# A hybrid decoder step: mixer work with 32-column products held for common slots, a fixed PE order, and two decay levels on all 128 keys

## The chip, the cores and the metric

The kernel runs on one core of a Trainium2 chip. The metric is the device time in microseconds (us), the median of several executions. Views of the profile come from one profiled execution. Engines: PE is TensorE's matmul and PEld its weight load, DVE is VectorE, ACT is ScalarE, POOL is GpSimd, SP is SyncE, which issues most of the DMAs. Matmuls of fp32 data appear in the trace as two instructions each.

## The reference, cut to what matters

A layer of a decoder on 256 prompt tokens and 8 new tokens of 8 samples (264 columns), with a model width of 2048:

```python
mod = jax.nn.silu(c) @ p['w_ada'][l] + p['b_ada'][l]
sh1, sc1, gt1, sh2, sc2, gt2 = jnp.split(mod[:, None, :], 6, axis=-1)
h = rmsnorm(x, p['g_pre_mix'][l]) * (1.0 + sc1) + sh1
z = h @ p['w_in'][l]
...
y_a = spatial_gating(u, v, sgu_w_s, sgu_b_s)                      # A
o_hg, S_hg = gated_linear_recurrence(q_hg, k_hg, hi, log_f, s_hg) # B: 8 heads, dk = dv = 128
o_g, S_g = gated_linear_recurrence(q_g, k_g, gv, log_a, s_gla)    # C: 4 heads, dk = 128, dv = 256
...
merged = gates[:, :, 0] * (branches[0] @ p['w_branch'][l, 0])     # and two more
out = merged @ p['w_out'][l]
x = x + gt1 * rmsnorm(out, p['g_post_mix'][l])
h2 = rmsnorm(x, p['g_pre_mlp'][l]) * (1.0 + sc2) + sh2
y2 = jnp.square(jax.nn.relu(h2 @ p['w_mlp_up'][l])) @ p['w_mlp_down'][l]
x = x + gt2 * rmsnorm(y2, p['g_post_mlp'][l])
```

The recurrence within a chunk is an attention matrix `att[t, s] = sum_d q[t, d] k[s, d] exp(b[t, d] - b[s, d])`, with `b` the running sum of the log decays. The outputs are the two activations, the final states of the prompts and the samples' updated states.

## The kernel before

All weights are fp32 in HBM and are streamed once, in blocks of 512 KB, through a ring of six buffers `raw` (L419 loads, three blocks ahead). A block is split in two parts, `whi` by a cast on ACT (L102) and `wlo` by a subtraction on DVE (L99). Its products with the split activations are three to a tile: L459, L460, L461, 128x128 weights by 264 columns; 24 of them make up one block, called a granule here. There are 13,872 of these main products in the program.

Beside them runs background work, written as Python generators that yield a cost after each step. `linear` calls three queues after each granule: `bg` with the mixers (A, then the two HGRN2 groups of four heads, then GLA), `bs` with the samples' state steps, `ba` with the rounds of the adaLN modulation. Each queue is pumped by a rate, so many steps to a granule:

```python
            bg.pump(rate[0])
            bs.pump(rate[1])
            ba.pump(rate[2])
```

The framework's scheduler then orders the instructions of each engine, PE's too, by its own estimates, within what data and buffers allow.

The pieces that the change touches:

- An adaLN step (`ada_round`, L265) multiplies the condition vectors by two blocks of `w_ada` of 512 KB each, in four products of 512 columns. They use the same `raw` ring. Of the two loads for the next step, one stands ahead of the step's products and one behind them.
- `mixer_r` builds the attention matrix by halving: five small levels within 32 tokens (`small_level`, L852, products of 32 keys by 32 queries), then halves of 32 (L908, 16 products of 32 by 32 a group) and of 64 (L916, 8 products of 64 by 64), then halves of 128 (L935). Behind that stand transposes of the keys (L942), the final states (L950, L951), the outputs (L973, L975, L976), each head's norm (L981, L987) and the transposes back to features (L995).
- `samples_r` advances the samples: it loads a state tile, scales it on ACT (L791), adds the outer product on DVE (L793), stores it from POOL's queue, and multiplies it by the query (L799, four products side by side in PE's column groups for HGRN2, two half sets for GLA).
- `finish(i)` drains what is left of a group and transposes the samples' outputs (L1008). `parts_b` calls it for the two HGRN2 groups, `parts_c` for GLA. `branch` calls these for its first tile, behind the projection of its gates (`zin`).

Of the kernel before, what the change touches and what calls it, by code (L numbers as in the profile page):

```python
# [15 lines left out]
P = 128  # L16
# [20 lines left out]
ST_BUFS = 3  # L37
# [9 lines left out]
FILL = (5.0, 9.0)  # L47


@with_exitstack  # L50
def hybrid_step_kernel(
# [53 lines left out]
    # ---------------------------------------------------------------- constants  # L105
# [7 lines left out]
    # ---------------------------------------------------------------- small vectors  # L113
# [7 lines left out]
    # x: prompt rows as two token tiles, the samples' feature tiles as rows  # L121
# [38 lines left out]
    # ---------------------------------------------------------------- norm helpers  # L160
    def rstd_small(ms, scale, out):
        """out = (ms * scale + EPS) ** -0.5, ms one piece or more of out's columns: a first guess from the exponent's bits, then Newton's steps to float32."""
        n, w = out.shape
        xx, aa = tmp([P, 16], "sx")[0:n, 0:w], tmp([P, 16], "sa")[0:n, 0:w]
        c = 0
        for m in ms if isinstance(ms, list) else [ms]:
            V.tensor_scalar(xx[:, c:c + m.shape[1]], m, scale, EPS, ALU.mult, ALU.add)
            c += m.shape[1]
        V.tensor_scalar(out.bitcast(I32), xx.bitcast(I32), -0.5, 1597463007.0, ALU.mult, ALU.add)
        for _ in range(3):  # L170
            mul(aa, out, out)
            V.scalar_tensor_tensor(aa, aa, -0.5, xx, ALU.mult, ALU.mult)
            V.scalar_tensor_tensor(out, aa, 1.5, out, ALU.add, ALU.mult)

    def sum_features(v, n, w):
        """Sums of v [P, n, w], which it overwrites, over its features (partitions and n tiles), on every partition."""
        while n > 1:
            n //= 2
            add(v[:, 0:n, :], v[:, 0:n, :], v[:, n:2 * n, :])
        ps = sm([P, w])  # L180
# [3 lines left out]
    # ---------------------------------------------------------------- x normed and transposed  # L184
    def norm_rows(x, xs, xsn, r):
        """r [P, 2] = the prompt rows' 1 / rms; xsn = the samples' rows xs [P, KT, NS] over their rms."""
# [7 lines left out]
        ps = sum_features(sq, KT, NS)  # L194
# [5 lines left out]
    def transposed(x, k):  # L200
        """Columns of feature tiles k and k + 1 of the prompt rows, in PSUM [P, 2, NP]."""
# [29 lines left out]
    # ---------------------------------------------------------------- adaLN  # L231
# [6 lines left out]
    def ada_rows(acc, n):  # L238
        """PSUM rows (32 j + c, columns) -> [P, i, j, c] with the columns' features on the partitions."""
        am = tmp([P, 512], "am", 1)  # L240
        S.copy(am[:, 0:n], acc[:, 0:n])
        ps = sm()
# [4 lines left out]
    def ada_round(r, pre=()):  # L247
        """Part r of the modulation; pre are its first blocks of weights."""
# [12 lines left out]
        for k in range(KT):  # L261
            if k + 1 < KT:
                ws.append(load(2 * k + 2))
            for j in range(4):
                T.matmul(acc[32 * j:32 * j + 32, :], cT[:, k, :], ws[j // 2][:, j % 2 * 512:j % 2 * 512 + 512], start=k == 0, stop=k == KT - 1)  # L265
            del ws[0:2]
            if k + 1 < KT:
                ws.append(load(2 * k + 3))
            yield
        rows = ada_rows(acc, 512)  # L270
        yield
        ch = slice(r * KT, (r + 1) * KT)
# [6 lines left out]

    class Queue:  # L280
        """Generators that advance a given number of steps, of any size, at a time."""

        def __init__(self):
            self.g, self.owed = [], 0.0

        def pump(self, n=1.0):
            self.owed += n
            while self.g and self.owed > 0.0:
                try:
                    c = next(self.g[0])  # L290
                    self.owed -= 1.0 if c is None else c
                except StopIteration:
                    self.g.pop(0)
            if not self.g:
                self.owed = 0.0

        def drain(self, gen=None):
            while self.g and (gen is None or gen in self.g):
                try:
                    next(self.g[0])  # L300
                except StopIteration:
                    self.g.pop(0)
# [24 lines left out]
    def ada_first(k0, n):  # L327
        """Shift and scale of the first sub-layer for n feature tiles, and those tiles' activations."""
# [18 lines left out]
        rows = ada_rows(acc, n * 64)  # L347
# [22 lines left out]
    # ---------------------------------------------------------------- streamed product  # L370
# [9 lines left out]
    def plan():  # L380
        """Every block of weights (matrix, row tile, row tiles, column, columns) in the order of use."""
# [28 lines left out]
    class Stream:  # L410
        """The blocks of weights, loaded LOAD_AHEAD and split SPLIT_AHEAD blocks before their products."""
# [36 lines left out]
    def granule(w, k0, n, c0, width, accs, xh, xl, k, first, last):  # L448
        """accs += (rows of w)^T @ x over n feature tiles: w's from k0 + k on, x's from k on, 256 columns to an acc."""
# [13 lines left out]

    def new_acc():
        return pmm.tile([P, 2, 512], F32, tag="mm", name=nm("mm"))

    def linear(w, k0, nk, c0, width, xh, xl):
        """PSUM tile [P, width // P, NT] = (rows k0.. of w, columns c0..c0+width)^T @ x."""
        acc = new_acc()
        kc = min(nk, 1024 // width)  # L470
        for kb in range(0, nk, kc):
            granule(w, k0, kc, c0, width, [acc], xh, xl, kb, kb == 0, kb + kc == nk)
            bg.pump(rate[0])
            bs.pump(rate[1])
            ba.pump(rate[2])
# [19 lines left out]
    # the first columns, by feature tiles as their activations become known  # L495
# [39 lines left out]
    def to_tokens(vt):  # L535
        """[P, 2, >= NP] feature rows of the prompt -> PSUM [P, t, m, P] token rows."""
# [6 lines left out]
    def rows_of(blks, prompt):  # L543
        """Feature rows (pairs of tiles) to the prompt's token rows: prompt(t, g) is the place of pair g."""
# [7 lines left out]
    def sample_rows(blks, eng=None):  # L552
# [7 lines left out]
        return ps  # L560

    # ---------------------------------------------------------------- A: spatial gating
    def mixer_a():
# [9 lines left out]
        for gg in range(2):  # L573
# [4 lines left out]
            mul(wsT[:, 4 * gg:4 * gg + 4, :], ps.rearrange("p (g n) -> p g n", g=4), triu.unsqueeze(1).to_broadcast([P, 4, P]))  # L578
        ps = sm()
# [18 lines left out]
        # the samples' rows, by feature  # L598
# [6 lines left out]
        ps = sum_features(w8, 8, NS)  # L605
# [4 lines left out]
        ps = sum_features(w8, 8, NS)  # L610
        yield 0.4
# [5 lines left out]
        V.tensor_copy(vbk.rearrange("p b k -> p k b"), vs)  # L617
        ps = sm([64, P])
        T.transpose(ps, vbk.rearrange("p b k -> p (b k)"), ident)
        yield 0.9  # L620
        so = tmp([64, P], "vso", 1)
# [9 lines left out]
        for gp in range(4):  # L631
# [14 lines left out]
            yield  # L646
    gen_a = mixer_a()
# [4 lines left out]
    def lower_bounds():  # L652
        """Logs of the lower bounds and of one less them."""
# [16 lines left out]
    def log_sigmoid(out, z, a):  # L670
        """out = log(sigmoid(z)), through a."""
# [9 lines left out]
    # ---------------------------------------------------------------- gated linear recurrences  # L681
# [7 lines left out]
    def hg_group(i):  # L689
        """Four HGRN2 heads."""  # L690
# [37 lines left out]
    def gla_group():  # L728
# [3 lines left out]
        wup = blk([16, 512])  # L732
# [8 lines left out]
        lr = tmp([16, NT], "lr", 1)  # L741
        S.copy(lr, z[0:16, 0, :])
        for m in range(4):
            ps = sm()
            T.matmul(ps[:, 0:NT], wup[:, m * P:(m + 1) * P], lr, start=True, stop=True)
            V.tensor_scalar(G.g[:, m, :], ps[:, 0:NT], bupT[:, m:m + 1], None, ALU.add)
        for s in range(4):
            z = zin(7168 + s * CW)
            S.copy(pair(G.v[s // 2], s % 2), z)
        G.s_in = lambda b, h, n: state_gla[0, b, h:h + n].rearrange("h k v -> k h v")  # L750
# [11 lines left out]
    def samples_r(G):  # L762
        """The samples' one step: S' = f S + k v^T, o = S'^T q."""
# [21 lines left out]
        os_ = tmp([P, dv], f"os{G.i}", 1)  # L785
        for n, (b, h0) in enumerate(steps):
# [7 lines left out]
            nc.gpsimd.dma_start(G.s_out(b, h0, nh), st)  # L794
            yield 0.5
            ps = sm([P, dv])
            for i in range(nh):
                h = h0 + i
                T.matmul(ps[32 * h:32 * h + 32, :], qm[:, h, b, :], st[:, i, :], start=True, stop=True)  # L799
            rs = slice(32 * h0, 32 * (h0 + nh))  # L800
            if b == 0:
                V.tensor_copy(os_[rs], ps[rs])
            else:
                add(os_[rs], os_[rs], ps[rs])
# [8 lines left out]
    def mixer_r(G):  # L813
# [10 lines left out]
        ps = sample_rows(G.v)  # L824
        yield 0.2
        vs = tmp([32 * nj, P], "vso", 1)
        S.copy(vs, ps)
# [10 lines left out]
        # prompts: decays by halving, every exponent at most 0  # L838
# [18 lines left out]

        ps = small_level(k, q)
        yield
        put_level(5, ps)  # L860
        for li, m in enumerate(LEVELS):
# [16 lines left out]
            yield  # L878
            ps = small_level(e, e)
# [7 lines left out]
        # halves of 32 and of 64  # L887
        for m in (32, 64):
# [13 lines left out]
            yield  # L902
            if m == 32:
                ps = sm([P, 8, 32])
                for h in range(4):
                    for b in range(4):
                        r_ = 64 * (b % 2)
                        T.matmul(ps[r_:r_ + 32, 2 * h + b // 2, :], e[:, h, 64 * b:64 * b + 32], e[:, h, 64 * b + 32:64 * b + 64], start=True, stop=True)  # L908
                yield
                S.copy(att[0:32, :, 32:64], ps[0:32])  # L910
                S.copy(att[64:96, :, 96:128], ps[64:96])
# [384 lines left out]
```

## Time and profile before

| | |
|---|---|
| median of 3 runs | 2009.66 us (2008.1 to 2011.21) |
| profiled execution, its span | 2009.9 us |
| PE busy | 1948.6 us (97%) |
| DVE busy, ACT busy | 1191.6 us (59%), 1002.0 us (50%) |
| DMA | 442.05 MB, 220 GB/s |
| main products L459, L460, L461 | 1332.1, 1321.9, 1317.3 us of PE, overlapping |
| adaLN steps L265 | 75.6 us of PE |
| stretch 270 to 980 us (mixers, branches) | PE busy 689.23 us, clock 0.98 |

Matmuls are pipelined, so busy times of groups on PE overlap and add up to more than the span. In a group's row stand the count, the busy time, the mean of one in ns, and the idle time of the engine ahead of it with what ended it. In a row of the timeline, the start and the length come first, and an idle time with its releaser may stand at the end in brackets.

### The profile page before, as it was taken

What the parts mean: (1) busy time and instruction counts of PE and PEld (TensorE: products, weight loads), DVE (VectorE), ACT (ScalarE), POOL (GpSimd) and SP (SyncE); (2) the same over time, 40 slices, a digit from 0 to 9 for tenths busy, and PEclk for the clock granted to TensorE, in tenths of its full rate; (3) what the DMA queues carried; (4) which work ended last, traced back from release to release, by engine and by line L of the source; (5) the groups of instructions that cost most, each with busy time, mean ns of one, the idle gap of its engine ahead of it and who ended that gap; (6) DMA issues with size and microseconds to landing.
All of it is one profiled execution on the core that took longest, in us unless ns stands there. A gap on an engine that the chain in (4) does not pass through costs nothing.

```text
span 2009.9 us, 42161 instructions
## 1 busy us (share of the span) xinstructions
PE 1948.6 (97%) x17020; PEld 1814.9 (90%) x17020; DVE 1191.6 (59%) x2105; ACT 1002.0 (50%) x1773; POOL 40.5 (2%) x66
## 2 busy tenths in 40 slices
PE   5999999999999999899899999999999999999997
PEld 4779898989988987789899995999999999999996
DVE  3456566777475687445555556555555555555656
ACT  4434354576664574454444445555444445454543
POOL 1000000000000000000000000000000000000000
PEclk9999999999999999999999999999999999999998
DMA  9887978787798668887555866655555555555552
GB/s 311 289 300 244 292 229 250 219 276 222 255 286 280 211 207 255 271 273 228 189 179 180 271 200 231 212 185 179 180 183 182 181 179 184 179 183 180 180 179 84
DMA packets 378179, 442.05 MB, mean 220 GB/s; under 512 B 14914, under 2 KB 339136, under 8 KB 377984
## 3 DMA queue, kind: packets, MB, share of 16 engines
q1 hardware_dynamic: 372592, 424.27, 66.7%
q0 software_dynamic: 4496, 13.90, 1.9%
q8 instruction: 133, 2.18, 0.4%
q10 hardware_dynamic: 896, 1.19, 0.2%
q14 instruction: 62, 0.51, 0.1%
HBM read 427.60 MB, written 11.70 MB: 219 GB/s over the span
## 4 chain that ended last, share of the span: by engine, by line
PE 91%; DMA 4%; DVE 2%; ACT 2%; issue 1%; SPq 0%; ACTq 0%; DVEq 0%
PE mm L459 28%; PE mm L460 27%; PE mm L461 27%; PE ada L265 3%; DMA st<-in_state_gla_dram 2%; PE ada L236 2%; DMA raw<-in_w_ada_dram 1%; PE sm L540 1%; PE sm L799 1%; DVE wlo L99 1%; ACT whi L102 1%; DMA raw<-in_w_in_dram 1%; PE sm L852 1%; DMA st<-in_state_hgrn_dram 0%; DMA b<-in_g_post_mix_dram 0%
## 5 line engine op out<-in xcount | busy, mean ns | idle before, releaser
L459 PE MATMUL mm<-b,whi 128*128 128x264 f32 x4624 | 1332.1, 288 | 17.3 <-ACT b L102 8.0
L460 PE MATMUL mm<-b,whi 128*128 128x264 f32 x4624 | 1321.9, 286 | 1.5 <-DVE b L99 1.5
L461 PE MATMUL mm<-b,wlo 128*128 128x264 f32 x4624 | 1317.3, 285 | 3.2 <-DVE wlo L99 3.2
L99 DVE TENSOR_TENSOR wlo<-raw,whi 128x512 fp32r<-128x512 f32 x1156 | 790.6, 690 | 654.1 <-ACT whi L102 616.3
L102 ACT CAST whi<-raw 128x512 fp32r<-128x512 f32 x1156 | 709.1, 619 | 799.5 <-PE mm L460 720.8
L459 PEld LDWEIGHTS mm<-b,whi 128*128 128x128 f32 x4624 | 873.4, 189 | 78.6 <-issue 31.4
L461 PEld LDWEIGHTS mm<-b,wlo 128*128 128x128 f32 x4624 | 872.8, 189 | 13.4 <-issue 7.2
L460 PEld LDWEIGHTS mm<-b,whi 128*128 128x128 f32 x4624 | 873.4, 189 | 11.4 <-issue 8.8
L96 DVE TENSOR_TENSOR b<-b,mm 128x528 f32<-128x528 f32 x136 | 94.9, 698 | 17.8 <-PE mm L461 17.7
L265 PE MATMUL ada<-raw,cT 128*32 128x512 f32 x464 | 75.6, 616 | 3.0 <-DMA raw<-in_w_ada_dram 3.0
L791 ACT ACTIVATE st<-st,fs 128x128 f32<-128x128 f32 (+1 forms) x96 | 37.0, 430 | 69.9 <-DMA st<-in_state_gla_dram 46.3
L793 DVE SCALAR_TENSOR_TENSOR st<-vbc,b,st 128x128 f32<-128x128 f32 (+1 forms) x96 | 33.9, 390 | 62.1 <-ACT st L791 49.0
L236 PE MATMUL ada<-raw,cT 128*32 128x256 f32 (+1 forms) x640 | 43.9, 359 | 3.0 <-DMA raw<-in_w_ada_dram 3.0
L93 DVE TENSOR_TENSOR b<-b,b 128x512 f32<-128x512 f32 (+1 forms) x47 | 33.7, 739 | 2.0 <-ACT b L869 1.6
L794 POOL DMA_DIRECT2D out_dram<-st x32 | 23.5, 736 | 411.0 <-DVE st L793 381.8
L236 PEld LDWEIGHTS ada<-raw,cT 128*32 128x32 f32 x640 | 14.8, 113 | 13.5 <-DMA raw<-in_w_ada_dram 3.7
L265 PEld LDWEIGHTS ada<-raw,cT 128*32 128x32 f32 x464 | 12.2, 110 | 15.7 <-DMA raw<-in_w_ada_dram 6.6
L99 DVE TENSOR_TENSOR b<-gt,b 128x528 fp32r<-128x528 f32 x32 | 22.6, 708 | 3.2
L93 DVE TENSOR_TENSOR gt<-vt 128x528 f32<-128x528 f32 x32 | 22.4, 700 | 0.0
L99 DVE TENSOR_TENSOR b<-b 128x1024 f32<-128x1024 f32 (+1 forms) x21 | 22.3, 1064 | 0.1
L1202 ACT ACTIVATE b<-vt 128x528 fp32r<-128x528 f32 x32 | 20.7, 647 | 1.0
L1196 ACT ACTIVATE vt<-mm 128x528 f32<-128x528 f32 x32 | 19.4, 607 | 0.0
(284 smaller groups left out, 729.5 us busy)
## 6 DMA issues: line engine op xcount, KB each, us to landing
raw<-in_w_in_dram SPq DMA_DIRECT2D x242, 512.0 KB, 5.3
raw<-in_w_ada_dram SPq DMA_DIRECT2D x164, 512.0 KB, 5.2
raw<-in_w_mlp_up_dram SPq DMA_DIRECT2D x128, 512.0 KB, 3.8
raw<-in_w_mlp_down_dram SPq DMA_DIRECT2D x128, 512.0 KB, 3.6
raw<-in_w_branch_dram SPq DMA_DIRECT2D x48, 512.0 KB, 5.1
raw<-in_w_out_dram SPq DMA_DIRECT2D x32, 512.0 KB, 4.3
raw<-in_w_ada_dram SPq DMA_DIRECT2D x32, 256.0 KB, 5.6
vbc<-vs_d SPq DMA_DIRECT2D x32, 256.0 KB, 6.7
```

The costliest lines, as they stand in the source:

```text
L93: V.tensor_tensor(o, a, b, op=ALU.mult)
L96: V.tensor_tensor(o, a, b, op=ALU.add)
L99: V.tensor_tensor(o, a, b, op=ALU.subtract)
L102: S.copy(hi, src)
L236: T.matmul(acc[32 * j:32 * j + 32, 0:n], cT[:, k, :], w[:, n * j:n * j + n], start=k == 0, stop=k == KT - 1)
L265: T.matmul(acc[32 * j:32 * j + 32, :], cT[:, k, :], ws[j // 2][:, j % 2 * 512:j % 2 * 512 + 512], start=k == 0, stop=k == KT - 1)
L459: T.matmul(o, a, xh(k + j), start=first and j == 0, stop=False)
L460: T.matmul(o, a, xl(k + j), start=False, stop=False)
L461: T.matmul(o, b, xh(k + j), start=False, stop=last and j == n - 1)
L791: S.activation(st[:, i, :], st[:, i, :], AF.Copy, scale=fs[:, h0 + i, b:b + 1])
L793: V.scalar_tensor_tensor(st[:, i, :], v[:, i, :], k[:, h0 + i, NP + b:NP + b + 1], st[:, i, :], ALU.mult, ALU.add)
L794: nc.gpsimd.dma_start(G.s_out(b, h0, nh), st)
```

## The change

PE's order is fixed from mixer A to the end of the third branch (`tc.manual_schedule`): PE runs the instructions in the order in which the program is written. The queues get two marks that a generator can yield. At READY it stops until at least one granule has gone by. At NARROW, ahead of products on 32 columns (small levels, sample steps), it stops until a slot comes:

```diff
+NARROW, READY = object(), object()
+SLOT_OWED = 1.0
+SLOT_LATE = 1.9
+SLOT_WAIT = 3
+HELD_OWED = 2.0
...
+    def background():
+
+        now[0] += 1
+        bg.pump(rate[0])
+        bs.pump(rate[1])
+        ba.owed = ba.owed + rate[2] if ba.g else 0.0
+        held = [q for q in (bg, bs) if q.open(NARROW)]
+        if ba.owed >= SLOT_LATE or held and (not ba.g or ba.owed >= SLOT_OWED or now[0] - min(q.at for q in held) >= SLOT_WAIT):
+            bg.slot()
+            bs.slot()
+            ba.pump(0.0)
...
         def pump(self, n=1.0):
             self.owed += n
-            while self.g and self.owed > 0.0:
...
+            while self.g and self.owed > 0.0 and (self.held is None or self.open(READY)):
+                self.step()
             if not self.g:
                 self.owed = 0.0
+            if self.held is not None:
+                self.owed = min(self.owed, HELD_OWED)
...
         for k in range(KT):
-            if k + 1 < KT:
-                ws.append(load(2 * k + 2))
             for j in range(4):
                 T.matmul(acc[32 * j:32 * j + 32, :], cT[:, k, :], ws[j // 2][:, j % 2 * 512:j % 2 * 512 + 512], start=k == 0, stop=k == KT - 1)
-            del ws[0:2]
-            if k + 1 < KT:
-                ws.append(load(2 * k + 3))
-            yield
...
+            ws = [load(2 * k + 2), load(2 * k + 3)] if k + 1 < KT else []
+            yield
...
-ST_BUFS = 3
+ST_BUFS = 4
...
+            sts.append(st)
             yield 0.5
+            if h0 + nh < 4:
+                continue
+            yield NARROW
             ps = sm([P, dv])
-            for i in range(nh):
-                h = h0 + i
-                T.matmul(ps[32 * h:32 * h + 32, :], qm[:, h, b, :], st[:, i, :], start=True, stop=True)
-            rs = slice(32 * h0, 32 * (h0 + nh))
+            for h in range(4):
+                T.matmul(ps[32 * h:32 * h + 32, :], qm[:, h, b, :], sts[h // nh][:, h % nh, :], start=True, stop=True)
...
+            yield READY
+            ps = sm([P, 8, 64])
+            for h in range(4):
+                for hf in range(2):
+                    b = e[:, h, P * hf:P * hf + P]
+                    rhs = b.rearrange("p (n j) -> p n j", j=2 * m)[:, :, m:2 * m]
+                    T.matmul(ps[:, 2 * h + hf, :].rearrange("p (n j) -> p n j", j=m), b, rhs, start=True, stop=True)
+            yield
             if m == 32:
-                ps = sm([P, 8, 32])
-                for h in range(4):
-                    for b in range(4):
-                        r_ = 64 * (b % 2)
-                        T.matmul(ps[r_:r_ + 32, 2 * h + b // 2, :], e[:, h, 64 * b:64 * b + 32], e[:, h, 64 * b + 32:64 * b + 64], start=True, stop=True)
...
         while not hasattr(G, "os"):
-            bs.pump(1.0)
+            bs.step()
...
         for m in range(8):
+            if m == 0:
+                yh, yl = parts()
             z = zin(9232 + n * D + m * CW)
             gt = tmp([P, 2, NT], "gt")
             S.activation(gt, z, AF.Tanh, scale=0.5)
-            if m == 0:
-                yh, yl = parts()
```

So the levels of 32 and of 64 now take eight products each, of all 128 keys by the 64 queries that need them (L961), and what is not needed is not copied. Both loads of an adaLN step's successor stand behind its products, and a slot runs adaLN steps (`ba.pump(0.0)`) as long as any are owed. Smaller edits: sums over partitions are cut in `fold` and `sum_partitions` with a hold between them, `sample_rows` copies its rows itself, `ada_rows` is cut in two, the products with `gla_w_up` are spread over the four projections behind them, and comments are gone. Outside of the fixed stretch the scheduler still sets PE's order.

How the instructions move, first on PE in the stretch of mixer A, about 2200 main products into the program. `raw` is a streamed block, `ada` the modulation's sums, `sm` a small PSUM tile, `mm` the main products' sums. Before:

```order
L636 MATMUL sm_4379<-b_3937,b_3865 128x128
L636 MATMUL sm_4379<-b_3937,b_3866 128x128
L265 MATMUL ada_3060<-raw_4223,cT 32x512 x2
L265 MATMUL ada_3060<-raw_4229,cT 32x512 x2
L459 MATMUL mm_4232<-b_2689,whi_4257 128x264
L460 MATMUL mm_4232<-b_2690,whi_4257 128x264
L461 MATMUL mm_4232<-b_2689,wlo_4258 128x264
```

And now:

```order
L486 MATMUL mm_4422<-b_1188,whi_4349 128x264
L487 MATMUL mm_4422<-b_1187,wlo_4350 128x264
L275 MATMUL ada_3060<-raw_4175,cT 32x512 x2
L275 MATMUL ada_3060<-raw_4177,cT 32x512 x2
L275 MATMUL ada_3060<-raw_4505,cT 32x512 x2
L275 MATMUL ada_3060<-raw_4507,cT 32x512 x2
L275 MATMUL ada_3060<-raw_4513,cT 32x512 x2
L275 MATMUL ada_3060<-raw_4515,cT 32x512 x2
L485 MATMUL mm_4422<-b_1852,whi_4403 128x264
```

Where one step stood between main products, three stand in a row here, on six blocks. The same place on SP, which issues the loads, with their waits. Before:

```order
L419 DMA raw_4209<-in_w_in_dram 128x4x256 [waits DMAHW5_49,DVE_49]
L256 DMA raw_4223<-in_w_ada_dram 128x1024 [waits DMAHW0_49,DVE_49]
L256 DMA raw_4229<-in_w_ada_dram 128x1024 [waits DMAHW6_49,PE_49]
L419 DMA raw_4265<-in_w_in_dram 128x4x256 [waits DMAHW7_49,PE_49]
L419 DMA raw_4335<-in_w_in_dram 128x4x256 [waits DMAHW1_49,DVE_49]
```

And now:

```order
L445 DMA raw_4497<-in_w_in_dram 128x8x128 [waits DMAHW6_49,DMAHW2_49,DVE_49]
L268 DMA raw_4505<-in_w_ada_dram 128x1024 [waits DMAHW7_49,DMAHW3_49,DVE_49]
L268 DMA raw_4507<-in_w_ada_dram 128x1024 [waits PE_49]
L268 DMA raw_4513<-in_w_ada_dram 128x1024 [waits PE_49]
L268 DMA raw_4515<-in_w_ada_dram 128x1024 [waits DMAHW0_49,DVE_49]
L268 DMA raw_4521<-in_w_ada_dram 128x1024 [waits DMAHW3_49,PE_49]
L268 DMA raw_4523<-in_w_ada_dram 128x1024 [waits DMAHW4_49,PE_49]
L445 DMA raw_4557<-in_w_in_dram 128x4x256 [waits DMAHW5_49,DMAHW1_49,PE_49]
```

Two adaLN loads stood between stream loads; now six stand in a row, each behind the readers of the buffer that it takes.

The third place is `parts_b` on PE, some 4300 main products into the program. Before:

```order
L461 MATMUL mm_8856<-b_2689,wlo_8886 128x264
L995 MATMUL sm_9026<-cst,b_8742 128x128 x4
L540 MATMUL sm_9034<-cst,b_3818 128x128 x4
L1008 MATMUL sm_9043<-cst,os_945_5497 128x128
L265 MATMUL ada_8946<-raw_8947,cT 32x512
L1008 MATMUL sm_9047<-cst,os_1266_7492 128x128
L540 MATMUL sm_9094<-cst,b_3818 128x128 x4
L265 MATMUL ada_8946<-raw_8947,cT 32x512
L265 MATMUL ada_8946<-raw_8949,cT 32x512 x2
```

Now, the beginning of what stands between two main products there (the rest are outputs, transposes and five sample steps, up to the second L1060):

```order
L487 MATMUL mm_8358<-b_2689,wlo_8388 128x264
L1060 MATMUL sm_8558<-cst,os_939_5417 128x128
L901 MATMUL sm_8562<-b_8469 32x32 x32
L901 MATMUL sm_8600<-b_8596 32x32 x32
L961 MATMUL sm_8645<-b_8638 128x64 x8
L961 MATMUL sm_8663<-b_8656 128x64 x8
L985 MATMUL sm_8683<-b_8674,b_8673 128x128 x4
L992 MATMUL sm_8690<-cst,b_8673 128x128 x4
L992 MATMUL sm_8696<-cst,b_8673 128x128 x4
```

Before, HGRN2 group 1 was down to its last transposes here; now the end of its chain, from the last two small levels on, stands between two main products.

More of the change, by code (lines that the diff above doesn't have):

```diff
@@ L346, in ada_first @@
             yield kn
-        rows = ada_rows(acc, n * 64)
+        rows = ada_rows(ada_am(acc, n * 64), n * 64)
         ni = n // 2
@@ L578, in mixer_a @@
             mul(wsT[:, 4 * gg:4 * gg + 4, :], ps.rearrange("p (g n) -> p g n", g=4), triu.unsqueeze(1).to_broadcast([P, 4, P]))
+        yield READY
         ps = sm()
@@ L604, in mixer_a @@
         V.tensor_copy(w8, vs)
-        ps = sum_features(w8, 8, NS)
+        fold(w8, 8)
+        yield READY
+        ps = sum_partitions(w8, NS)
         yield 0.3
@@ L609, in mixer_a @@
         mul(w8, vs, vs)
-        ps = sum_features(w8, 8, NS)
-        yield 0.4
+        fold(w8, 8)
+        yield 0.3
+        yield READY
+        ps = sum_partitions(w8, NS)
+        yield 0.1
         rstd_small(ps, 1.0 / BW, r8)
@@ L646, in mixer_a @@
             yield
+    order = tc.manual_schedule(engines={mybir.EngineType.PE})
+    order.__enter__()
     gen_a = mixer_a()
@@ L931, in mixer_r @@
         yield
+        yield READY
         attx = blk([P, 4, P])
@@ L944, in mixer_r @@
             yield
+        yield READY
         for h0 in range(0, 4, nh):
@@ L988, in mixer_r @@
             yield
+        yield READY
         o = [blk() for _ in range(nj)]
@@ L1100, in hybrid_step_kernel @@
     branch(2, lambda: parts_c(gates_c))
+    order.__exit__(None, None, None)
     ba.drain()
```

89 lines of the change are left out of this document (50 added, 39 removed).

## The prediction, as put on record before the changed kernel ran

> **What bounds the kernel now.** I read the page first: busy times and the chain that ended last.
>
> ```profile
> span 2009.9 us, 42161 instructions
> PE 1948.6 (97%) x17020; PEld 1814.9 (90%) x17020; DVE 1191.6 (59%) x2105; ACT 1002.0 (50%) x1773; POOL 40.5 (2%) x66
> PE 91%; DMA 4%; DVE 2%; ACT 2%; issue 1%; SPq 0%; ACTq 0%; DVEq 0%
> ```
>
> PE is busy 97% of the span and carries 91% of the chain. The other engines matter only where PE waits for them. Next, the windows of the stretch where mixers, branches and adaLN steps run beside the main products (columns: stretch, length, then PE, PEld, DVE, ACT, POOL busy, clock, DMA share, GB/s).
>
> ```profile
> 270.00:980.00 710.00, 689.23 (x6614) 617.18 (x6613) 455.03 (x863) 394.75 (x763) 31.47 (x46) 0.98 0.78 248
> ```
>
> Here PE idles 21 us in 710 and the clock is 0.98, so almost nothing is left to win by removing waits. The timeline shows what a switch from the main products to other work costs. I measure from the last main product ahead to the fifth behind.
>
> ```profile
> 479.63 0.28 PE L461 MATMUL mm<-b,wlo 128*128 128x264 f32 x1
> 479.84 0.42 PE L799 MATMUL sm<-st,b 128*32 128x128 f32 x8
> 480.80 0.29 PE L460 MATMUL mm<-b,whi 128*128 128x264 f32 x1
> ...
> 489.94 0.28 PE L461 MATMUL mm<-b,wlo 128*128 128x264 f32 x1
> 490.15 0.42 PE L799 MATMUL sm<-st,b 128*32 128x128 f32 x8
> 490.39 1.04 PE L265 MATMUL ada<-raw,cT 128*32 128x512 f32 x8
> 491.97 0.29 PE L460 MATMUL mm<-b,whi 128*128 128x264 f32 x1
> ...
> 272.04 0.28 PE L461 MATMUL mm<-b,wlo 128*128 128x264 f32 x1
> 272.25 1.07 PE L265 MATMUL ada<-raw,cT 128*32 128x512 f32 x8
> 273.85 0.29 PE L460 MATMUL mm<-b,whi 128*128 128x264 f32 x1
> ```
>
> From 273.85 on, main products start 0.1215 us apart (68 intervals to 282.02). Less five of those (0.61), a sample step alone costs 1.17 - 0.61 = 0.56 us, an adaLN step alone 1.20, both in one excursion 2.03 - 0.61 = 1.42. One excursion saved is worth 0.56 + 1.20 - 1.42 = 0.34 us. That is all that common slots can bring per merge.
>
> Last, idle rows and what they do to the clock:
>
> ```profile
> 652.48 0.59 PE L459 MATMUL mm<-b,whi 128*128 128x264 f32 x1 [3.60 <-ACT whi L102]
> 789.07 0.39 PE L459 MATMUL mm<-b,whi 128*128 128x264 f32 x1 [2.41 <-ACT whi L102]
> 853.03 2.08 PE L950 MATMUL sm<-b,b 128*128 128x256 f32 x4 [3.72 <-ACT b L943]
> 974.93 0.49 PE L459 MATMUL mm<-b,whi 128*128 128x264 f32 x1 [3.91 <-ACT b L102]
> ...
> 650.80:657.60 6.80, 5.12 (x22) 4.89 (x23) 4.54 (x9) 4.85 (x11) 1.06 (x2) 0.50 0.59 192
> 790.70:794.10 3.40, 3.40 (x76) 3.10 (x75) 2.37 (x6) 1.50 (x3) 0.45 (x1) 0.51 0.98 306
> 852.20:859.00 6.80, 5.97 (x20) 3.05 (x20) 4.65 (x8) 3.14 (x7) 1.03 (x2) 0.50 0.69 229
> 975.10:981.90 6.80, 4.59 (x17) 3.69 (x18) 2.73 (x3) 1.07 (x1) 1.38 (x3) 0.50 0.66 218
> ```
>
> Each idle stretch of 2.41 us or more is followed by 3.40 or 6.80 us at a clock of 0.50. What is lost is half of PE's busy time there: 2.56, 1.70, 2.99 and 2.30 us, mean 2.4.
>
> **The change part by part.** The fixed order puts work into slots between two granules (24 main products, 2.9 us). I take the profiled execution's 2009.9 us as base; the median of 2009.66 is the same within 0.01%.
>
> *Two or three adaLN steps in one slot.* The slot's last call runs adaLN steps while any are owed, and the new `ada_round` issues a step's two loads only behind the products of the step before. In the order, 13 slots hold a second step, four of them a third: 17 steps with no main product between them and the step that precedes their loads. The loads' waits are on PE's products of the same slot, or on DVE's split of a block two granules ahead, which is done about as late. Nothing covers the landing. How long that is:
>
> ```profile
> raw<-in_w_ada_dram SPq DMA_DIRECT2D x94, 512.0 KB, 4.9
> ...
> 1216.05 3.50 DMA raw<-in_w_ada_dram
> 1219.60 1.04 PE L265 MATMUL ada<-raw,cT 128*32 128x512 f32 x2 [2.71 <-DMA raw<-in_w_ada_dram]
> ```
>
> The first line is the median of the stretch (4.9 us from issue to landing), the second a load issued into a just-freed buffer (3.50, from the chain of waits), for which PE idled 2.71. A first step's products end 1.28 us behind the last main product's start (272.25 + 1.07 + the pipeline's end, less 272.04); with 3.5 to 4.9 us on top the second can start at 4.8 to 6.2 instead of about 1.06: 3.7 to 5.1 idle. I take 4.3: 13 x 4.3 = 56 us (bounds 3.4 and 5.2 each: 44 to 68). A third step needs another 1 MB; at the 306 GB/s of the window from 790.70 that is 3.5 us, less 0.9 that PE works: 4 x 2.6 = 10 (6 to 14). Each of the 13 idles longer than the 2.41 us above, so each is followed by half clock: 13 x 2.4 = 31 (at 1.7 to 3.0 each: 22 to 39).
>
> In the Trainium skill, "TensorE: Matmul & The Clock Gate", section "Part 1: The HAM clock gate", the clock is said to drop after at least one idle window of about 3.4 us and to come back after one busy window. By that rule one busy window is 3.4 us, 1.7 lost per slot, and the sum would be 9 us less. The rows differ: 6.80 us at half clock in three of four, and a drop after 2.41 us idle.
>
> *Drains.* PE now stands still where `parts_b` calls `finish(0)` and `finish(1)`: all that is left of HGRN group 1 (two 32-column levels, the two wide ones, transposes, states, outputs, norm, five sample steps) lies in order between two main products; `parts_c` does this with GLA's outputs. In the trace of before these steps had main products beside them. Durations, by form:
>
> ```profile
> L93 DVE TENSOR_TENSOR b<-b,b 128x1024 f32<-128x1024 f32 x3 | 3.7, 1219 | 0.4 <-ACT b L925 0.4
> L978 ACT COPY b<-sm 128x512 f32<-128x512 f32 x8 | 4.7, 584 | 3.2 <-PE sm L976 2.1 <-PE sm L973 1.1
> L981 ACT ACTIVATE junk<-b 128x128 f32<-128x128 f32 x16 | 5.0, 309 | 0.5
> L987 ACT ACTIVATE b<-b,rr 128x128 f32<-128x128 f32 x16 | 5.4, 393 | 0.5 <-DVE rr L173 0.5
> L793 DVE SCALAR_TENSOR_TENSOR st<-vbc,b,st 128x128 f32<-128x128 f32 x64 | 19.3, 345 | 20.2 <-ACT st L791 14.8 <-DMA raw<-in_w_ada_dram 5.5
> L799 PE MATMUL sm<-st,b 128*32 128x256 f32 x64 | 10.4, 405 | 0.0
> ```
>
> HGRN: about nine DVE passes at 1.22 lead to the decayed keys (11 us); transposes, copies and states to 18; two output halves, each with a copy (0.58) and four squares (0.31), to 23; the rstd's chain of small operations 2; eight scales (0.39) to 28; the last state loads and steps, norm and transposes of the samples to 39. PE's own work in it is 13: 26 idle, and one stretch of half clock, 2.4. GLA: the same tail from the outputs on, 23 less 10 of PE's work: 12.5, and 2.4. Together 43. Bounds: 25 if ACT and DVE overlap twice as well as I chained them, 57 if the state loads queue behind the stream's. Five shorter waits in the order (a step's operand made in the same granule) I put at 0.9 each: 4.5 (3 to 6).
>
> *What it saves.* Runs of work of other column widths between main products fall from 176 to 124: 52 x 0.34 = 17.7. GLA's sample products no longer come in halves: 16 sets of two took 10.4 us (last row); 8 sets of four, at twice the columns of the 0.42 us set at 479.84, take 6.7: 3.6. Idle that goes: the READY hold gives the wait at 853.03 a granule (3.72 + 2.99 = 6.7); `parts()` ahead of the branch's first projection lets that projection cover the split awaited at 974.93 (3.91, another 2.21 idle within the half-clock window, 2.30 lost: 8.4); of the two waits for ACT's cast at 652.48 and 789.07 (3.60 + 2.56 + 2.41 + 1.70 = 10.3 with the clock) I take half, 5 (0 to 10.3).
>
> *The two levels.* Prices the same way:
>
> ```profile
> 486.19 0.28 PE L461 MATMUL mm<-b,wlo 128*128 128x264 f32 x1
> 486.40 0.70 PE L908 MATMUL sm<-b 128*32 128x32 f32 x32
> 487.62 0.29 PE L460 MATMUL mm<-b,whi 128*128 128x264 f32 x1
> ...
> 497.21 0.28 PE L461 MATMUL mm<-b,wlo 128*128 128x264 f32 x1
> 497.42 1.15 PE L916 MATMUL sm<-b 128*64 128x64 f32 x16
> 499.09 0.29 PE L460 MATMUL mm<-b,whi 128*128 128x264 f32 x1
> ...
> 523.55 0.28 PE L461 MATMUL mm<-b,wlo 128*128 128x264 f32 x1
> 523.68 1.05 PE L973 MATMUL sm<-b,att 128*128 128x128 f32 x8
> 525.06 0.28 PE L460 MATMUL mm<-b,whi 128*128 128x264 f32 x1
> ```
>
> The old levels cost 0.82 and 1.27, without an excursion 0.48 + 0.93 = 1.41. Four 128-key products (x8: two passes each) cost 0.90; sixteen new ones 3.6 (at least 1.9, at the second row's rate). Three groups: 3 x 2.2 = +6.6 (+1.4 to +6.6).
>
> **Sum:** 56 + 10 + 31 + 43 + 4.5 + 6.6 - 17.7 - 3.6 - 6.7 - 8.4 - 5 = +110: 2120 us. All low ends: 44 + 6 + 22 + 25 + 3 + 1.4 - 17.7 - 3.6 - 6.7 - 8.4 - 10.3 = +55; all high ends, with the savings on excursions halved and the ACT waits kept: 68 + 14 + 39 + 57 + 6 + 6.6 - 8.9 - 3.6 - 6.7 - 8.4 = +163.
>
> **The rivals.**
> 1. *Faster: the loads are there.* If the second steps' loads are issued a landing (4.9 us) ahead of their slots, they cost nothing, and the sample steps and mixer tails of the drains would have been advanced early too: the savings alone stay, 6.6 - 41.4 = -35: 1975. It decides where a buffer comes free two granules (5.8 us) before the slot. For it: a granule less of waiting would cover most of a landing. Against: in the order these loads wait for that slot's own products. Chance 0.05.
> 2. *Idle, but at full clock.* If the clock survives stretches of 3 to 5 us, the 31 and the 5 behind the drains go: 2084. For: the half clock lasts 3.40 in one of the rows and 6.80 in the others, so more than the idle time decides. Against: 2.41 us of idle were enough. Chance 0.14. The skill's rule above, with a window whose edges run free, would let some slots escape like this.
> 3. *The burst delays the stream.* Four or six loads of 512 KB in a row on SP's queue stand ahead of the stream's next block. The stretch already moves 248 GB/s, and the block two ahead would arrive a granule late after each of 13 slots: 13 x 2.9 = 38 more, 2158. Against: a stall of 4.3 us gives the stream that time back. Chance 0.14.
>
> My sum keeps 0.67. The forecast is its 2120. The range, 2050 to 2170, reaches from the lower half of rival 2 (its own low end is 2065 less the 22 us of half clock, 2043) past rival 3's 2158 to the sum's high end. A change of 0.2% (4 us) is what a measurement of this kernel can tell. Faster 0.05 is rival 1; the same 0.01; slower 0.94.
>
> **What would show it.** PE idle ahead of L275's second steps of 3.5 to 5 us at 13 places, released by the adaLN load, each with 3.4 or 6.8 us at clock 0.50; one hole of some 39 us in the main products in `parts_b` and one of 23 in `parts_c`; the new level line L961 at 3 x 3.6 us. I am wrong if L275's idle is below 20 us, if the drains hold less than 20 of idle, or if the clock of the stretch stays at 0.98.

## The result

The changed kernel takes 2131.6 us (median of 4 runs, 2123.0 to 2136.7) against 2008.9 us of the kernel before: 1.060 times as long, 95% interval 1.057 to 1.063. The forecast was 2120 us, range 2050 to 2170, slower with 0.94.

From the page of the changed kernel, its span, its busy line and the row of the adaLN steps, and below that the row of the adaLN steps in the kernel before:

```profile
span 2134.8 us, 42024 instructions
PE 1992.1 (93%) x16972; PEld 1838.7 (86%) x16972; DVE 1191.0 (56%) x2097; ACT 1006.2 (47%) x1773; POOL 40.5 (2%) x66
L275 PE MATMUL ada<-raw,cT 128*32 128x512 f32 x464 | 103.7, 699 | 60.1 <-DMA raw<-in_w_ada_dram 60.1
...
L265 PE MATMUL ada<-raw,cT 128*32 128x512 f32 x464 | 75.6, 616 | 3.0 <-DMA raw<-in_w_ada_dram 3.0
```

PE's share falls from 97 to 93% although it executes fewer instructions; DVE and ACT are busy about as long as before. The adaLN steps (L275) wait 60.1 us for their loads, where L265 in the kernel before waited 3.0.

Nearly all of the difference, 121.9 of the 124.9 us between the two traces, lies between the 1393rd and the 7000th main product. The windows of that stage, first of the kernel before, then of the changed one (stretch, length, busy PE, PEld, DVE, ACT, POOL, clock, DMA share, GB/s):

```profile
257.59:1113.16 855.57, 834.80 (x7803) 762.75 (x7802) 538.31 (x984) 464.84 (x874) 31.47 (x46) 0.99 0.75 236
```

```profile
259.30:1236.85 977.55, 874.60 (x7756) 784.26 (x7754) 537.47 (x976) 469.50 (x874) 31.48 (x46) 0.94 0.68 206
```

The stage is 122 us longer. PE idles 103.0 instead of 20.8 us in it, and is busy 40 us longer at a lower mean clock, with 47 instructions fewer.

One slot, with three steps in a row, in the timeline of PE:

```profile
390.47 0.28 PE L487 MATMUL mm<-b,wlo 128*128 128x264 f32 x1
390.68 1.07 PE L275 MATMUL ada<-raw,cT 128*32 128x512 f32 x8
391.99 1.05 PE L275 MATMUL ada<-raw,cT 128*32 128x512 f32 x4 [0.24 <-DMA raw<-in_w_ada_dram]
395.63 1.05 PE L275 MATMUL ada<-raw,cT 128*32 128x512 f32 x4 [2.59 <-DMA raw<-in_w_ada_dram]
397.21 3.17 PE L275 MATMUL ada<-raw,cT 128*32 128x512 f32 x8 [0.52 <-DMA raw<-in_w_ada_dram]
400.31 0.51 PE L485 MATMUL mm<-b,whi 128*128 128x264 f32 x1
```

The first step (x8) runs at once. The second comes in two halves (x4 and x4): the load of the later half was issued only at 391.77, behind the first step's products, and landed at 395.59, so PE idles 2.59 us ahead of that half. The third takes 3.17 us instead of 1.05: the load of its second half lands at 398.41, and the clock has been halved since 397.17. Main products, 0.12 us apart otherwise, stand still for 9.8 us.

The drain of HGRN2 group 1 in `parts_b`, the rows of PE that begin with a wait and the two ends:

```profile
750.07 0.27 PE L1060 MATMUL sm<-cst,os 128*128 128x128 f32 x1
...
752.83 2.00 PE L961 MATMUL sm<-b 128*128 128x64 f32 x16 [1.24 <-DVE b L1061]
756.90 3.65 PE L961 MATMUL sm<-b 128*128 128x64 f32 x16 [2.07 <-DVE b L98]
763.55 2.08 PE L985 MATMUL sm<-b,b 128*128 128x128 f32 x8 [3.01 <-DVE b L98]
...
778.61 0.48 PE L1047 MATMUL sm<-cst,b 128*128 128x128 f32 x1 [5.09 <-ACT b L1038]
...
785.95 1.47 PE L850 MATMUL sm<-st,b 128*32 128x128 f32 x8 [2.64 <-DVE st L841]
790.85 0.48 PE L1060 MATMUL sm<-cst,os 128*128 128x128 f32 x1 [3.44 <-ACT os L860]
```

From 750 to 791 us no main product runs: 41 us, of which PE idles 18.4. The later levels' decays on DVE, the scales on ACT (L1038) and the samples' last state and norm each hold PE up.

### The profile page after: what moved, and what is told of

Its sections match the earlier page's. It is cut to its first block, busy times and chain, and to the rows that moved or that the text cites. A ratio compares the mean times of both kernels' runs of the same rounds, so it can differ in the third digit from the quotient of the medians.

```text
span 2134.8 us, 42024 instructions
## 1 busy us (share of the span) xinstructions
PE 1992.1 (93%) x16972; PEld 1838.7 (86%) x16972; DVE 1191.0 (56%) x2097; ACT 1006.2 (47%) x1773; POOL 40.5 (2%) x66
## 4 chain that ended last, share of the span: by engine, by line
PE 52%; DMA 2%; ACT 1%; DVE 1%; issue 0%; SPq 0%; DVEq 0%; ACTq 0%
PE mm L485 16%; PE mm L486 16%; PE mm L487 16%; PE ada L275 1%; DMA st<-in_state_gla_dram 1%; DMA raw<-in_w_ada_dram 1%; PE sm L576 0%; DVE b L1291 0%; PE sm L850 0%; PE sm L215 0%; ACT junk L1032 0%; PE sm L1047 0%; ACT whi L107 0%; DVE wlo L104 0%; PE sm L1198 0%
## 5 line engine op out<-in xcount | busy, mean ns | idle before, releaser
L486 PEld LDWEIGHTS mm<-b,whi 128*128 128x128 f32 x4624 | 879.4, 190 | 9.1 <-issue 8.0
L275 PE MATMUL ada<-raw,cT 128*32 128x512 f32 x464 | 103.7, 699 | 60.1 <-DMA raw<-in_w_ada_dram 60.1
L101 DVE TENSOR_TENSOR b<-b,mm 128x528 f32<-128x528 f32 x136 | 95.0, 698 | 17.8 <-PE mm L487 17.7
L275 PEld LDWEIGHTS ada<-raw,cT 128*32 128x32 f32 x464 | 15.8, 115 | 103.1 <-DMA raw<-in_w_ada_dram 96.6
```

Source lines behind the costliest of these rows:

```text
L101: V.tensor_tensor(o, a, b, op=ALU.add)
L486: T.matmul(o, a, xl(k + j), start=False, stop=False)
```

## The experiments

For every kernel I split the stage between the same two main products into three: PE's idle time (the gaps between its rows), the loss to half clock (half of PE's busy time in the records of a clock of 0.5), and the rest. Ratios are against the kernel before, on the same chip; its medians lay between 2008.6 and 2011.0 us.

| kernel | time, us | ratio (95%) | stage | idle | half clock | rest |
|---|---|---|---|---|---|---|
| before | 2009 to 2011 | 1 | 855.6 | 20.8 | 9.6 | 825.2 |
| changed | 2131.6 | 1.060 (1.057 to 1.063) | 977.5 | 103.0 | 46.3 | 828.3 |
| one step to a slot | 2037.2 | 1.013 (1.012 to 1.015) | 878.5 | 38.4 | 17.7 | 822.4 |
| loads as before | 2129.3 | 1.058 (1.056 to 1.061) | 973.2 | 100.3 | 45.1 | 827.8 |
| both of these | 2035.8 | 1.013 (1.011 to 1.015) | 879.4 | 39.7 | 17.1 | 822.7 |
| no fixed order | 2073.8 | 1.032 (1.030 to 1.033) | 918.1 | 55.3 | 21.4 | 841.4 |
| before + fixed order | 2019.7 | 1.005 (1.004 to 1.006) | 864.6 | 28.6 | 13.8 | 822.3 |
| before + fixed order + steps in a row | 2132.8 | 1.061 (1.059 to 1.063) | 973.6 | 92.5 | 42.6 | 838.4 |
| before + wide levels | 2011.8 | 1.0013 (1.0003 to 1.0024) | 855.8 | 18.5 | 5.8 | 831.5 |
| one step, high rates | 2024.4 | 1.008 (1.006 to 1.009) | 862.3 | 31.6 | 9.6 | 821.1 |
| the same, slots after one granule | 2027.3 | 1.009 (1.008 to 1.010) | 872.3 | 34.0 | 14.1 | 824.3 |
| the same, old levels | 2021.4 | 1.007 (1.005 to 1.008) | 865.4 | 32.9 | 13.6 | 819.0 |
| best of all, middle rates | 2019.3 | 1.005 (1.003 to 1.007) | 864.9 | 35.2 | 13.5 | 816.2 |
| the same, state update on POOL | 2035.8 | 1.013 (1.011 to 1.016) | 882.0 | 47.6 | 14.2 | 820.3 |

**One adaLN step to a slot.**

```diff
-            ba.pump(0.0)
+            if ba.g and ba.owed > 0.0:
+                ba.step()
```

> The changed kernel (2131.6 us) with at most one adaLN step in a slot; the holds, the fixed PE order and the place of the loads stay. My theory (second and third steps of a slot wait for loads that cannot start before the slot, 57 us of PE idle, and the clock halves behind them): the waits at the adaLN step's line go from 60 to under 10 us, the loss to half clock falls from 54 to about 25, the drain of the HGRN groups is shorter because slots come oftener (66 products in it instead of 142), 20 more excursions of PE cost 7: about 2045 us. Rival (the fixed order as such is what costs, the idle goes to the next wait in line): 2100 us or more, with the idle at other lines.

2037.2 us. The wait at the adaLN line in its page:

```profile
L275 PE MATMUL ada<-raw,cT 128*32 128x512 f32 x464 | 73.8, 606 | 6.2 <-DMA raw<-in_w_ada_dram 6.2
```

One line of the change's code carries 94 of its 123 us. Idle falls by 65, 54 of it at this line and the most of the others in the drain, which is shorter because slots come oftener; half clock falls by 29. The idle did not come back elsewhere, so the fixed order as such is not the main cause.

**Before's place of the loads.**

```diff
+            if k + 1 < KT:
+                ws.append(load(2 * k + 2))
             for j in range(4):
                 T.matmul(acc[32 * j:32 * j + 32, :], cT[:, k, :], ws[j // 2][:, j % 2 * 512:j % 2 * 512 + 512], start=k == 0, stop=k == KT - 1)
-            ws = [load(2 * k + 2), load(2 * k + 3)] if k + 1 < KT else []
+            del ws[0:2]
+            if k + 1 < KT:
+                ws.append(load(2 * k + 3))
```

> The changed kernel with before's place of the adaLN loads: one of the next step's two loads ahead of the step's products, one behind. Several steps in a slot stay. My theory: the second of the two blocks still cannot start before the slot's first step has ended, so the second steps stay late by about as much and the third steps get another landing: 2115 to 2145 us, idle at the adaLN line 45 to 75. Rival (the place of the loads is the cause, not the steps in a row): idle at the adaLN line under 25, 2070 us or less.

> The changed kernel with at most one adaLN step in a slot and before's place of the loads. My theory: where no step follows another in a slot, nothing is left for an earlier load to hide: within 8 us of the kernel with one step to a slot alone (about 2045 us). Rival (loads behind the products are late for slots one granule apart as well): 10 us or more below that kernel.

With steps in a row kept: 2129.3 us, and the adaLN line still waits 57.7 us. With one step to a slot: 2035.8 against 2037.2. The place of the loads costs nothing that these runs can tell; the steps in a row cost.

**No fixed order.** Both lines of `tc.manual_schedule` are taken out.

> The changed kernel without the fixed PE order; the framework's scheduler orders PE, the program order with holds and slots stays. My theory: the scheduler puts main products between a late step and the one before it and into the drains, so idle of PE falls from 125 to about 60 us and half clock from 54 to about 20; excursions go back from 62 to 106: about 2025 to 2050 us. Rival (the slots themselves and the wide levels cost, whatever the order): 2100 us or more.

2073.8 us: between the two, and a miss. The scheduler does put main products between late steps, but it places a step's first half and second half apart:

```profile
429.28 0.28 PE L487 MATMUL mm<-b,wlo 128*128 128x264 f32 x1
429.49 1.05 PE L275 MATMUL ada<-raw,cT 128*32 128x512 f32 x4
430.47 0.39 PE L485 MATMUL mm<-b,whi 128*128 128x264 f32 x1
...
431.40 1.05 PE L275 MATMUL ada<-raw,cT 128*32 128x512 f32 x4
```

Half a step (x4) takes the 1.05 us of a whole one (x8), and main products stand between the halves of 17 of the stage's 48 steps. So the rest of the stage rises to 841.4, and 35.3 us of waits for loads stay. My theory had not counted the halves.

**The fixed order alone, and steps in a row put into the kernel before.** The first adds only `tc.manual_schedule` to the kernel before; the second adds to that the two parts under suspicion:

```diff
-            ba.pump(rate[2])
+            ba.owed = ba.owed + rate[2] if ba.g else 0.0
+            if ba.owed >= 1.9:
+                ba.pump(0.0)
...
+            ws = [load(2 * k + 2), load(2 * k + 3)] if k + 1 < KT else []
```

> The kernel before with one thing added: PE's order fixed to the program's order over the same stretch, without holds, slots or anything else of the change. My theory (the fixed order costs only where the program order puts steps behind one another that wait): the order shows 12 places where PE reaches a step with nothing between it and what it waits for, 17 in the kernel before, so within 6 us of the kernel before (2009 us). Rival (the scheduler's free order is worth much, since a fixed one cannot give way when DVE, ACT or a load is late): 2025 us or more.

> The kernel before with the fixed order and two things of the change: adaLN steps run when 1.9 are owed, several in a row, and both loads of a step stand behind the products of the step before. No holds, no wide levels. The order has 16 places with 24 steps whose loads cannot start earlier, against 13 and 17 in the changed kernel. My theory, with the changed kernel's measured idle of 57/17 = 3.35 us a step and 2.3 us of half clock a place: 24 x 3.35 + 16 x 2.3 = 117 us above the fixed order alone, less 3 for ten excursions fewer: about 2123 us. Rival (the loss in the changed kernel needs the holds and the crowded slots; steps in a row alone are covered): under 2060 us.

The fixed order alone costs 10 us (2019.7): idle +7.8, half clock +4.2, rest -2.9. That is more than the 6 I allowed and less than the rival's. The additional idle is not at the main products, whose own waits in the stage are 16.8 us instead of 16.5. Most of it is ahead of mixer A's products (L619 4.1, L580 2.2 us), which wait for DVE. Steps in a row then add 113 us (2132.8) where 114 were expected. The page's line:

```profile
L263 PE MATMUL ada<-raw,cT 128*32 128x512 f32 x464 | 111.1, 711 | 74.6 <-DMA raw<-in_w_ada_dram 74.6
```

They need no holds or crowded slots to cost this. The rest rises by 16.1 us with ten excursions fewer (3.4): 19.5 us for 24 steps, 0.8 us a step which is neither idle nor half clock. The timeline shows what it is: 25 of the stage's 48 steps run their two halves apart here, as in the slot shown above, 2 in the kernel with the fixed order alone. Such a step keeps PE busy for 1.90 us (time at half clock counted half), a whole one for 1.08: 25 x 0.82 = 20.5 us.

**The wide levels alone.** The edit of L961 in the kernel before.

> The kernel before with one thing changed: the levels of 32 and of 64 as eight products each of all 128 keys. My theory (PE bound there, four products of all keys cost 0.90 us): three groups x (3.6 - 1.41) = 6.6 us more, 0.33%: 2016 us. Rival (the wide products spare a change of the array's tile and lie in gaps anyway): no change or up to 3 us less.

2011.8 us, 0.13% more (0.03 to 0.24). In the trace the rest of the stage rises by 6.3 us, the forecast 6.6. The idle and the half clock were 6.1 us lower in this execution, so that the median rises by 3 us only, less than the 6.6 expected. The runs don't tell whether the change causes that or the clock's chance. One set of eight products in the changed kernel:

```profile
568.71 0.29 PE L487 MATMUL mm<-b,wlo 128*128 128x264 f32 x1
568.83 1.90 PE L961 MATMUL sm<-b 128*128 128x64 f32 x16
570.53 0.37 PE L485 MATMUL mm<-b,whi 128*128 128x264 f32 x1
```

**The drains.** On top of one step to a slot, rates of (2.2, 2.2, 2.2, 1.0) for the mixers and (0.25, 0.45, 0.35, 0.2) for the samples; then `SLOT_WAIT` of 1 instead of 3; then the old levels too.

> The kernel with one adaLN step to a slot (2037 us) with higher rates for the mixers and the samples (2.2 a granule instead of 1.7 and 1.5; 0.25, 0.45, 0.35, 0.2 for the samples), so that the groups are finished before the branches ask for them: no transposes, states or outputs are left between two main products of parts_b and parts_c. My theory (what is left of the loss is mostly the two drains: idle of 10 and 3 us with their half clock, and the waits for split activations behind them): 15 to 22 us less, about 2018 us. Rival (the work of the drain only moves to other places where PE waits for it just as well): 2030 us or more.

> As the kernel with the higher rates, with slots that open after one granule instead of three. 90 excursions of PE between main products instead of 83: 7 x 0.34 = 2 us more than that kernel, if an excursion saved is worth 0.34 us as my theory has it. Rival (an excursion saved is worth a granule's wait or more, 1 us): 7 us more or above.

> As the kernel with the higher rates and slots after one granule, with the levels of 32 and 64 as before the change (16 products of 32 by 32 and 8 of 64 by 64). My theory: 6 us less than with the wide levels, less the two mixed excursions more: about 2013 us, level with the kernel before. Rival (wide levels are free): the same as with the wide levels.

Without a drain 2024.4 us, 12.8 less than with it where 15 to 22 were expected; 7 us of idle come back at one place, where PE reaches the states (L1002) ahead of ACT. Slots after one granule cost 2.9 more, within what the runs can tell of the 2 expected. The old levels give 5.9 us back (6 expected); with the shortfall of the first step, the 2013 us expected of this version are missed by 8.

**The best of all.** One step to a slot, the loads and the levels as before, rates (1.9, 1.9, 1.7, 1.0) for the mixers and (0.22, 0.42, 0.32, 0.15) for the samples.

> All that the runs so far point to: one adaLN step to a slot, before's place of the loads, the levels of 32 and 64 as before, and rates (1.9, 1.9, 1.7 for the mixers) at which the order shows no drain left, less high than the 2.2 at which PE waited 7 us for the states of a group. My theory: the rest of the stage as at the best (819 us), idle between the kernel before's 21 and 30 us, half clock about 10: 2008 to 2016 us. Rival (holds and slots save nothing that a fixed order does not lose): 2018 us or more.

2019.3 us, outside of what I expected and the rival's case. The rest is the lowest of all, 816.2: 9.0 below the kernel before. Idle and half clock take 18 back. A piece of the chain of waits shows where (start, length, what):

```profile
792.52 10.35 DMA st<-in_state_gla_dram
...
803.39 0.49 ACT st L844
803.88 0.52 ACT whi L107
...
804.45 0.59 PE mm L489
```

ACT stands at the scale of a sample's state until the state has landed, and the cast that the main products need is queued behind it.

**The state update on POOL.**

```diff
-            for i in range(nh):
-                S.activation(st[:, i, :], st[:, i, :], AF.Copy, scale=fs[:, h0 + i, b:b + 1])
-            for i in range(nh):
-                V.scalar_tensor_tensor(st[:, i, :], v[:, i, :], k[:, h0 + i, NP + b:NP + b + 1], st[:, i, :], ALU.mult, ALU.add)
+            nc.gpsimd.tensor_tensor(st, st, fs[:, h0:h0 + nh, b:b + 1].to_broadcast([P, nh, dv]), ALU.mult)
+            nc.gpsimd.tensor_tensor(v, v, k[:, h0:h0 + nh, NP + b:NP + b + 1].to_broadcast([P, nh, dv]), ALU.mult)
+            nc.gpsimd.tensor_tensor(st, st, v, ALU.add)
```

> The last version (one adaLN step to a slot, old levels, middle rates; 2019 us) with the samples' state update taken from ACT and DVE to POOL, as three operations on the whole tile. In the last version's trace ACT waits for the samples' state loads up to 11.1 us at a time, with the casts of the streamed blocks queued behind. My theory (these waits are what makes the main products wait for ACT's casts, 16.9 us in the stage): PE's idle in the stage falls from 35 to about 20, half clock from 13.5 to about 8: about 2000 us, below the kernel before. Rival (the casts are late for other reasons, or POOL's operations slow DVE down or end too late for the branches): 2015 us or more.

2035.8 us. Half of the theory held: the main products' wait for ACT's casts in 300 to 1080 us falls from 16.9 to 4.1. But the subtraction on DVE became slower. Its group, POOL's longest, and the products that wait for the subtraction and for the adaLN loads, in this kernel over the same stretch:

```profile
L104 DVE TENSOR_TENSOR wlo<-raw,whi 128x512 fp32r<-128x512 f32 x401 | 311.0, 790 | 255.0 <-ACT whi L107 245.1 <-PE mm L490 6.5
L845 POOL TENSOR_TENSOR st<-st,vbc 128x512 f32<-128x512 f32 x32 | 49.9, 1561 | 1.9
L491 PE MATMUL mm<-b,wlo 128*128 128x264 f32 x1601 | 461.2, 288 | 21.8 <-DVE wlo L104 21.4
L277 PE MATMUL ada<-raw,cT 128*32 128x512 f32 x360 | 56.1, 604 | 14.7 <-DMA raw<-in_w_ada_dram 14.7
```

And in the kernel without it:

```profile
L104 DVE TENSOR_TENSOR wlo<-raw,whi 128x512 fp32r<-128x512 f32 x412 | 279.1, 690 | 212.5 <-ACT whi L107 204.5 <-PE mm L490 4.5 <-PE mm L491 0.2
L491 PE MATMUL mm<-b,wlo 128*128 128x264 f32 x1647 | 472.4, 287 | 7.3 <-DVE wlo L104 7.3
L277 PE MATMUL ada<-raw,cT 128*32 128x512 f32 x360 | 51.0, 608 | 4.2 <-DMA raw<-in_w_ada_dram 4.2
```

The mean goes from 690 to 790 ns. Only subtractions that run beside an operation of POOL are slower: 66 of them, with a median of 1350 ns, against 689 ns on average for the 334 others. The main products now wait 21.4 us for the subtraction instead of 7.3, and the adaLN steps 14.7 us for their loads instead of 4.2. What makes these loads later was not tried. The rival was right. No version tried beats the kernel before.

## Why the prediction was right

The forecast is 12 us below the measured median, and its mechanism holds: adaLN steps in a row, whose loads can't have started. By the steps of the sum, each from the profiled execution of the changed kernel:

- *Steps in a row:* 66 us forecast, 57 found (60.1 less the 3.0 that the kernel before has as well). The third steps were too dear: their loads are issued beside the second's, and in one slot both steps follow a single wait of 5.80 us.
- *Half clock:* forecast 31 behind the slots and 4.8 behind the drains, less 7.4 that went with saved waits, 28; found 36.7 in the stage. In 12 of 13 slots or behind them the clock halves, for 68 us in all. In the drains it halves for 44 us with what follows them, where I had put one stretch each. By the Trainium skill's rule, one window of 3.4 us a slot, the sum came out 9 us lower: 3.41 us stands behind six slots, 6.83 or 10.24 behind six, nothing behind one. That every stretch of half clock in this stage lasts a multiple of 3.41 us agrees with the window of the Trainium skill's "TensorE: Matmul & The Clock Gate", section "Part 1: The HAM clock gate". Read as a window that is idle throughout, the page's "idle window" does not agree: two waits of 1.21 and 1.56 us, with 1.05 us of products between them (837 to 841 us), were followed by half clock.
- *Drains:* 26 and 12.5 us of idle forecast, 18.4 and 10.8 found. PE's own work in the first took 23 us instead of 13. The clock stood at half for 26 of the 41 us, and 14.4 us of the work fell there, so half clock makes 7 of these 10 us. The hole is 41 us long, 39 were forecast.
- *Excursions and levels:* this term failed. Forecast -17.7 - 3.6 + 6.6 = -14.7, found +3.1 in the rest of the stage. The levels cost what was forecast (6.3 in the rest of the stage where they stand alone, 5.9 us back where they are taken out). The prices per excursion come near where nothing stalls: -9.0 in the best version, with 24 fewer, old levels and whole sample sets, where the prices make it -11.8. What I put at nothing is that a step whose blocks land one after the other runs its two halves apart. All 17 second and third steps do so, their halves starting 1.25 to 4.25 us apart instead of 0.45, and each keeps PE busy for 1.86 us (time at half clock counted half) instead of 1.06: 17 x 0.8 = 13.6 us, less 3.5 for four such steps in the kernel before. That is 10 of the 17.8 us that the term is off; the other 8 stay open.
- *Idle that goes:* the 3.7 us ahead of the states are gone, and so are the main products' waits for split activations, 6.1 us in the stage before (4.6 for ACT, 1.5 for DVE). But their waits for the split blocks of weights, of which I took a part away, rise from 10.4 to 14.2 us (9.2 for ACT's cast, 5.0 for the subtraction). The five shorter waits, put at 4.5 us, are 2.6 us of idle at most, all that is left beside slots, drains and the main products' own waits.

In all, idle was forecast to rise by 96 us and rose by 82, half clock by 28 and 37, the rest by -15 and +3. That errors of -14, +8 and +18 leave only 12 us is partly luck. In the prediction's price of an excursion, the 68 intervals are 67, of 0.122 us; the five that it takes off are 0.61 us either way.

Rival 1 (loads there in time) and rival 2 (full clock) are excluded by the 57 and the 36.7 us. Rival 3 (the stream late by a granule a slot, 38 us) is not seen: the main products wait only 3.8 us longer for split blocks than before.

## What to carry to other kernels

Before steps are gathered to save switches, price the switch (0.34 us here) against the landing of the load that the next step needs (3.5 to 5 us): gathering pays only for steps whose data is there already. A load that is issued behind its predecessor's products needs other work between the two, and a count of main products between a step and what releases it, taken from the instruction order, finds the places ahead of time. A stall costs more than its length: here 82 us of additional idle brought 37 us of half clock, and each late step ran its halves apart for another 0.8 us.

## What was not expected of the hardware

- Two products of an adaLN step alone take 1.05 us, as long as all four: splitting a step in halves doubles its cost, and a load that lands late for one half is enough to split it.
- Elementwise work on POOL (three operations of 1.3 to 1.6 us a tile) slows DVE's subtractions from 690 to 790 ns on average, those that run beside it to a median of 1350 ns, although the subtraction and POOL's operations share no data.
- A fixed PE order without any other change costs 10 us, 0.5%, although by my count its order has fewer places than the free one (12 against 17) where PE reaches a step with nothing between it and what it waits for.
